# Decode attention by plain fp32 matmuls on four 32-column tiles instead of rounded/rest pairs

## The chip, the core and the metric

The kernel runs on one NeuronCore of a Trainium2 chip. The metric is the device time of one launch in microseconds (us). PE is the matrix engine (TensorE); PEld are its weight loads, which can overlap its matmuls. DVE, ACT and POOL are the vector, scalar and general engines, SP only issues transfers. PE reads from SBUF, where tensors lie on 128 partitions, and writes to PSUM, which has 8 banks of 512 fp32 columns on each partition.

## What is computed

One inference step of a hybrid decoder layer for 256 prompt tokens and 8 decode sequences (one new token each, 2048 tokens in the past). The part that the change touches is the attention of the decode tokens; there are 8 heads in 2 groups of 4, and each group shares one key/value head of 128 numbers.

```python
# compressed branch -> scores of 64-token blocks -> top 16 of them
o_slc = slc_sample(q, kv_slc, cache_slc, page_table, idx, valid, ...)  # 15 past blocks of 64 keys + the new token
o_win, _ = dense_gqa(q, kv_all[:, :, 0], kv_all[:, :, 1], mask, d, slopes)  # the last 512 keys + the new token
# each branch, per head: s = q.k * SCALE - slope * distance; p = softmax(s); o = p @ v
o = g[:, :, 0] * o_cmp + g[:, :, 1] * o_slc + g[:, :, 2] * o_win
y_a = (o * silu(z_a)) @ w_pa
```

The rest of the layer is one large projection of all 264 tokens, compression of the caches, prompt attention, a gated delta rule, and two output projections.

## The kernel before

**The stream of projections.** Most of PE's work is a list `halves` of half units: a 512 KB piece of weights is loaded by SP into a `raw` buffer (4 halves ahead, 3 buffers), split by ACT and DVE into a rounded part `hi` and a rest `lo` (2 halves ahead), and multiplied by the likewise split activations in three matmuls of 264 columns for each of 8 pieces: hi·hi, hi·rest, rest·hi (`three`, tile `acc`). Their operands have the type fp32r, in which one matmul is one pass over the array. A plain fp32 matmul is two records in the trace, and so two weight loads.

**The side work.** Everything else is written as generators. After each half of a half unit (12 matmuls of the stream) `tick` lets every active generator go on to its next `yield`; `yield 3` skips three ticks. Prompt attention (`g_attn`), the decode chain (`g_dec_cmp`, then `g_dec_slc`, then `g_dec_win`), and later the delta rule are such generators. SP and POOL issue in the order of the program; for PE, ACT and DVE the tile framework's scheduler sets the order by its own simulated times, so that side work stands between the matmuls of the stream. PE takes its instructions in the order in which they were written.

**Decode attention, selected branch (`g_dec_slc`).** For each of 8 sequences two indirect transfers on POOL's queue gather 120 rows of 4 KB of keys (tile `gk`), later of values (`gv`); the next sequence's are asked for one sequence ahead. PE transposes the keys (`gtr`), and ACT and DVE take them out of PSUM as a rounded part and a rest (`gkx`). The queries lie in `qm` the same way: 16 blocks, one for each of the 2 heads' groups and 8 sequences, in each of which only the four rows of that group and sequence are not zero. So every matmul adds into all 64 rows (2 groups x 8 sequences x 4 heads) of one score tile `gsc`: `qk` gives one matmul with 128 query columns (rounded and rest) on the rounded keys, and one with 64 on the keys' rest. `scores` adds both halves of the partitions, `row_softmax` works on 64 partitions, `pt_split` transposes the 64 rows of probabilities and splits them again (`sP`). `split1` splits the values (`gvx`), and `pv_part` multiplies: 2 matmuls of 256 columns (both groups' values) for each of 8 key tiles; `pv_take` adds from the result `pvo` only the rows that belong to this group and sequence (a mask `rmask`) to `acc2`.

**Decode attention, window branch (`g_dec_win`).** The same with 512 keys per sequence that come by plain transfers on SP's queue, for two sequences at a time (`wk`, `wv`), and go out again, shifted by a token, to the output cache on POOL's queue (`o_wk`, `o_wv`). Their splits are `wkx` and `wvx`, the scores `wsc`, the probabilities `wP`. At the end two small matmuls (`smo`) bring `acc2` into the order of the output.

All large tiles (`gk`, `gkx`, `gv`, `gvx`, `wk`, `wkx`, ...) share 13 buffers of one pool (`slot`): a new tile waits until the last reader of the tile that had its buffer is done.

Of the kernel before, what the change touches and what calls it, by code (L numbers as in the profile page):

```python
# [10 lines left out]
F32 = mybir.dt.float32  # L11
# [37 lines left out]

def shape_constants():  # L50
# [14 lines left out]
    for t in range(2):  # L65
# [8 lines left out]
    row = np.arange(64)  # L74
    srow = slope[(row // 32) * 4 + row % 4]
    c.add("c64", srow[:, None] * np.arange(64)[None])
    c.add("wrow", srow[:, None] * (np.arange(8) * 64 - 512)[None])
    c.add("e64", (row[None] // 4) == np.arange(16)[:, None])
    c.add("sel", ((row[None, None] // 32) == np.arange(2)[None, :, None])
          & (((row[None, None] // 4) % 8) == np.arange(8)[:, None, None]))  # L80
    c.add("rmask", ((p[:, None] % 64) // 4) == np.arange(16)[None])
# [57 lines left out]
def program(tc, A):  # L139
# [37 lines left out]
    # constants  # L177
# [41 lines left out]
    # long-lived small tiles  # L219
# [14 lines left out]
    grow = cp.tile([64, 2], F32, name="grow")  # L234
# [37 lines left out]
    # ---- x: rms norm, split  # L272
# [36 lines left out]
    # ---- streams  # L309
# [167 lines left out]
    # ---- projections  # L477
# [17 lines left out]
    def g_qstat(h):  # L495
# [7 lines left out]
        if h == 7:  # L503
# [19 lines left out]
            L["qm"] = qm = slot("qm", [128, 2112], F32R)  # L523
            G.memset(qm.bitcast(F32), 0.0)
            qv = qm.rearrange("p (i c) -> p i c", c=132)
            qf = qd.rearrange("p g b r -> p (g b) r")
            S.activation(qv[:, :, 0:4], qf, AF.Copy)
            V.tensor_sub(qv[:, :, 64:68], qf, qv[:, :, 0:4])
# [63 lines left out]
    def g_small(ps):  # L592
# [25 lines left out]
        S.activation(gd, p2[:, 0:64], AF.Copy)  # L618
        for br in range(2):
            mm(p2[0:64, 192 + br:193 + br], x[:, 2 + 2 * br:4 + 2 * br].rearrange("p a b r -> p (a b r)"), ones[0:24, 0:1])  # L620
        V.tensor_copy(grow, p2[0:64, 192:194])
# [8 lines left out]
    # ---- decode: compressed attention, selection, gathers  # L630
    def g_dec_cmp():
# [42 lines left out]
        # ranks  # L674
# [44 lines left out]
        mm(p7[0:64, 0:16], C("e64", 16), vb[:, 1, :])  # L719
        sb_ = cp.tile([64, 16], F32, name="sbias")  # L720
        V.tensor_scalar(sb_, p7[0:64, 0:16], 64.0, -float(PAST), ALU.mult, ALU.add)
        V.tensor_scalar(sb_, sb_, C("c64", 64)[:, 1:2], None, ALU.mult)
# [4 lines left out]
    def new_token(w):  # L727
        yield from wait("q")
        pr = tp.tile([128, 64], F32, name="ntp", tag="a", bufs=NA)
        V.tensor_tensor(pr.rearrange("p (g b r) -> p g b r", g=2, b=NB), qd,  # L730
                        knT[:, w, :, :, None].to_broadcast([128, 2, NB, 4]), ALU.mult)
        yield 3
        pt = psb("ntk")
        mm(pt[0:64, 128:129], pr, ones[:, 0:1])
        for g in range(2):
            mm(pt[0:64, 0:128], C("sel", 8)[:, 64 * g:64 * g + 64], L["kvd"][:, w, 1, g, :], start=g == 0, stop=g == 1)
        sn = tp.tile([64, 8], F32, name="ntm", tag=f"ntm{w}")
        ve = tp.tile([64, 128], F32, name="ntv", tag=f"ntv{w}")
        V.tensor_scalar(sn[:, 0:1], pt[0:64, 128:129], SCALE, None, ALU.mult)
        S.activation(ve, pt[0:64, 0:128], AF.Copy)  # L740
        L["nt", w] = sn, ve
        mark(("nt", w))

    def row_softmax(sc, n, w):
# [11 lines left out]
        V.scalar_tensor_tensor(acc2[0:64], ve, sn[:, 4:5], acc2[0:64], ALU.mult, ALU.add)  # L756

    def scores(out, sc, bias, shape):
        lo = slot("slo", [64, 960])
        lo = lo[:, 0:math.prod(shape)]  # L760
        for k, ps in enumerate(out):
            n = math.prod(shape) // len(out)
            S.activation(lo[:, n * k:n * k + n], ps[64:128, 0:n], AF.Copy, scale=SCALE)
            V.scalar_tensor_tensor(sc[:, n * k:n * k + n], ps[0:64, 0:n], SCALE, lo[:, n * k:n * k + n], ALU.mult, ALU.add)
        V.tensor_add(sc, sc, bias)

    def qk(ps, i, hi, lo, first, last):
        qm = L["qm"]
        a, b = qm[:, 128 * i:128 * i + 128], qm[:, 128 * i:128 * i + 64]
        n = hi.shape[-1]  # L770
        if first:
            mm(ps[:, 0:n], a, hi, start=True, stop=False)
        mm(ps[0:64, 0:n], b, lo, start=False, stop=False)
        if not first:
            mm(ps[:, 0:n], a, hi, start=False, stop=last)

    def pt_split(name, sc, nt, np_):
        pt = psb("ptr")
        for t in range(nt):
            tr(pt[0:np_, 64 * t:64 * t + 64], sc[:, np_ * t:np_ * t + np_])  # L780
        P_ = slot(name, [128, 8, 128], F32R)
        v = pt[0:np_, 0:64 * nt].rearrange("p (t c) -> p t c", t=nt)
        S.activation(P_[0:np_, 0:nt, 0:64], v, AF.Copy)
        V.tensor_sub(P_[0:np_, 0:nt, 64:128], v, P_[0:np_, 0:nt, 0:64])
        return P_

    def pv_part(po, P_, np_, ts, nt, hi, lo):
        for t in ts:
            h = lambda: mm(po[:, 0:256], P_[0:np_, t, :], hi(t), start=t == 0, stop=t == nt - 1)
            if t == 0:  # L790
                h()
            mm(po[0:64, 0:256], P_[0:np_, t, 0:64], lo(t), start=False, stop=False)
            if t:
                h()

    def pv_take(po, b):
        for g in range(2):
            i = 8 * g + b
            V.scalar_tensor_tensor(acc2, po[:, 128 * g:128 * g + 128], C("rmask")[:, i:i + 1], acc2, ALU.mult, ALU.add)

    def split1(name, src, shape, np_=128):
        x = slot(name, [128, 2] + shape, F32R)
        S.activation(x[0:np_, 0], src, AF.Copy)
        V.tensor_sub(x[0:np_, 1], src, x[0:np_, 0])
        return x

    def g_dec_win():
# [30 lines left out]
        def wk_qk(b, x):  # L838
            for g in range(2):
                qk(ps, 8 * g + b, x[:, 0, g], x[:, 1, g], b + g == 0, b * g == 7)  # L840

        prev = None
        for b in range(NB):
            if b % 2 == 0:
                if b < 6:
                    load_k(b // 2 + 1)
                else:
                    load_v(0)
            x = split1("wkx", kr[b // 2][:, b % 2, :, 0:512], [2, 512])
            if prev is not None:  # L850
                yield 3
                wk_qk(b - 1, prev)
            prev = x
        yield 2
        wk_qk(7, prev)
        bb = slot("wb", [64, 2, 512])
        V.tensor_tensor(bb[:, 0].rearrange("p (n m) -> p n m", m=64), C("wrow", 64)[:, :, None].to_broadcast([64, 8, 64]),
                        C("c64", 64)[:, None, :].to_broadcast([64, 8, 64]), ALU.add)
        sc = bb[:, 1]
        yield 7  # L860
        scores([ps], sc, bb[:, 0], [512])
# [3 lines left out]
        P_ = pt_split("wP", sc, 4, 128)  # L865
        def wv_pv(b, x):
            po = PV("pvo")
            pv_part(po, P_, 128, range(4), 4, lambda t: x[:, 0, t], lambda t: x[:, 1, t])
            pv_take(po, b)

        prev = None
        for b in range(NB):
            if b % 2 == 0 and b < 6:
                load_v(b // 2 + 1)
            x = split1("wvx", vr[b // 2][:, b % 2], [4, 256])
            if prev is not None:
                yield
                wv_pv(b - 1, prev)
            prev = x
        yield 5  # L880
        wv_pv(7, prev)
        yield 7
        pt = psb("smo")
        yield 2
        for i in range(2):
            mm(pt[:, 0:64], acc2, ident[:, 64 * i:64 * i + 64], start=i == 0, stop=i == 1)
        V.tensor_add(oD, oD, pt[:, 0:64])
        mark("oD")

    def g_dec_slc():  # L890
        yield from wait("idx")
        yield from wait(("kv", 0), 4)
        G.memset(acc2, 0.0)
# [15 lines left out]
        def gk_qk(b, g, x):  # L909
            for half in range(2):  # L910
                o = slice(480 * half, 480 * half + 480)
                qk(ps[half], 8 * g + b, x[:, 0, o], x[:, 1, o], b + g == 0, b * g == 7)

        prev = None
        for b in range(NB):
            if b < NB - GP:
                kr[b + GP] = gather("gk", "cslk", b + GP)
            elif b - NB + GP < VP:
                vr[b - NB + GP] = gather("gv", "cslv", b - NB + GP)
            for g in range(2):  # L920
                x = slot("gkx", [128, 2, 960], F32R)
                for half in range(2):
                    pt = psb("gtr")
                    for t in range(4):
                        tr(pt[:, 120 * t:120 * t + 120], kr[b][0:120, g, 4 * half + t, :])
                    o = slice(480 * half, 480 * half + 480)
# [3 lines left out]
                if prev:  # L930
                    gk_qk(*prev)
                prev = b, g, x
            del kr[b]
        yield 6
# [785 lines left out]
```

## Time and profile before

| | us |
|---|---|
| median of 3 runs (1165.35 to 1169.48) | 1166.74 |
| profiled execution, span | 1167.3 |
| PE busy | 1135.1 (97%) |
| PE weight loads busy | 1097.8 (94%) |
| DVE busy | 789.7 (68%) |
| ACT busy | 607.6 (52%) |
| POOL busy | 147.5 (13%) |

The page gives no time outside the span, and the span of the profiled execution lies within the spread of the timed runs. A share of busy time is an average over stages; matmuls overlap in their records (one ends while the next has begun), so that what a matmul takes of PE is the distance from its start to the next start, and not its own length. The decode chain's selected branch stands between 388 and 571 us, its window branch between 560 and 664 us.

### The profile page before, as it was taken

How to read it: one execution, taken by the hardware profiler on the slowest of the kernel's cores; microseconds unless marked ns; L12 is line 12 of the kernel's file. 1: busy time of each engine (PE TensorE's matmuls, PEld its weight loads, DVE VectorE, ACT ScalarE, POOL GpSimd, SP SyncE). 2: the span in 40 equal slices, each digit the busy share in tenths (PEclk: the TensorE clock that was granted, in tenths of full speed). 3: DMA queues.
4: the chain of work that ended last, by engine and by line, in shares of the span. 5: the costliest groups of instructions: out<-in, count | busy, mean ns of one | idle time of the engine just before them, and what ended most of it. 6: DMA issues, size and time to landing. Idle time of an engine off the chain costs nothing.

```text
span 1167.3 us, 24685 instructions
## 1 busy us (share of the span) xinstructions
PE 1135.1 (97%) x9136; PEld 1097.8 (94%) x9136; DVE 789.7 (68%) x1651; ACT 607.6 (52%) x1173; POOL 147.5 (13%) x218
## 2 busy tenths in 40 slices
PE   3999999999999999999899999998999999999998
PEld 3989999999999997998899999998998799999998
DVE  3487665443677876986888876899575665567543
ACT  4455655444635776875666554443345354344332
POOL 4420344100001221204112100100100000000000
PEclk9999999999999999999999999999999999999999
DMA  8874576334436865468887644554743345555663
GB/s 296 256 223 148 191 217 203 106 133 164 159 133 198 227 181 147 135 192 210 320 316 269 245 162 162 188 204 134 231 172 118 127 145 179 183 181 210 206 237 128
DMA packets 76844, 222.83 MB, mean 191 GB/s; under 512 B 10465, under 2 KB 27370, under 8 KB 75186
## 3 DMA queue, kind: packets, MB, share of 16 engines
q1 hardware_dynamic: 59922, 168.55, 42.7%
q0 software_dynamic: 14784, 45.68, 13.6%
q10 hardware_dynamic: 2016, 7.01, 1.5%
q8 instruction: 72, 1.18, 0.4%
q14 instruction: 50, 0.41, 0.1%
HBM read 203.21 MB, written 17.99 MB: 189 GB/s over the span
## 4 chain that ended last, share of the span: by engine, by line
PE 82%; DVE 5%; DMA 3%; issue 1%; POOL 1%; ACT 1%; SPq 0%; DVEq 0%; ACTq 0%; POOLq 0%
PE acc L199 66%; PE og L199 2%; DMA gv<-cslv,idx 2%; DVE lo L327 1%; DVE lanes L1234 1%; PE po L199 1%; PE gsc L199 1%; PE gtr L196 1%; PE sw L199 1%; DVE prod L1233 1%; PE ps L199 1%; PE pvo L199 1%; DMA raw<-win 1%; PE dS L199 1%; PE cf L199 1%
## 5 line engine op out<-in xcount | busy, mean ns | idle before, releaser
L326 ACT ACTIVATE hi<-raw 128x1024 fp32r<-128x1024 f32 (+1 forms) x250 | 264.1, 1056 | 324.2 <-PE acc L199 260.5
L199 PE MATMUL acc<-xh,hi 128*128 128x264 f32 (+1 forms) x1488 | 428.5, 288 | 1.4 <-DVE gate L1489 1.0
L199 PE MATMUL acc<-xl,hi 128*128 128x264 f32 (+1 forms) x1488 | 426.6, 287 | 0.0
L199 PE MATMUL acc<-xh,lo 128*128 128x264 f32 (+1 forms) x1488 | 425.9, 286 | 0.0
L327 DVE TENSOR_TENSOR lo<-raw,hi 128x1024 fp32r<-128x1024 f32 (+1 forms) x250 | 304.5, 1218 | 172.1 <-ACT hi L326 168.5
L199 PEld LDWEIGHTS acc<-xh,hi 128*128 128x128 f32 (+1 forms) x1488 | 280.3, 188 | 3.8 <-ACT hi L326 1.2
L199 PEld LDWEIGHTS acc<-xl,hi 128*128 128x128 f32 (+1 forms) x1488 | 280.4, 188 | 1.9 <-issue 0.7
L199 PEld LDWEIGHTS acc<-xh,lo 128*128 128x128 f32 (+1 forms) x1488 | 279.5, 188 | 2.0 <-issue 1.0
L199 PE MATMUL acc<-hi,w1h 128*128 128x254 f32 (+1 forms) x512 | 147.6, 289 | 16.5 <-ACT hi L403 16.5
L199 PE MATMUL acc<-lo,w1h 128*128 128x254 f32 (+1 forms) x512 | 146.4, 286 | 3.8 <-DVE lo L404 3.6
L199 PE MATMUL acc<-hi,w1l 128*128 128x254 f32 (+1 forms) x512 | 144.9, 283 | 0.0
L404 DVE TENSOR_TENSOR lo<-rawc,hi 128x512 fp32r<-128x512 f32 (+2 forms) x136 | 84.0, 656 | 51.1 <-ACT hi L403 45.3
L199 PEld LDWEIGHTS acc<-hi,w1h 128*128 128x128 f32 x512 | 97.8, 191 | 16.8 <-ACT hi L403 16.7
L403 ACT ACTIVATE hi<-rawc 128x512 fp32r<-128x512 f32 (+2 forms) x136 | 74.6, 599 | 58.6 <-PE acc L199 54.4
L199 PEld LDWEIGHTS acc<-lo,w1h 128*128 128x128 f32 x512 | 98.3, 192 | 5.1 <-DVE lo L404 4.9
L199 PEld LDWEIGHTS acc<-hi,w1l 128*128 128x128 f32 x512 | 98.3, 192 | 0.1
L380 POOL DMA_DIRECT2D rawc<-ccmp x125 | 67.4, 539 | 100.4 <-issue 70.0
L199 PE MATMUL acc<-oh,hi 128*128 128x264 f32 x256 | 72.9, 285 | 0.4 <-ACT gate L1482 0.4
L199 PE MATMUL acc<-ol,hi 128*128 128x264 f32 x256 | 72.7, 284 | 0.0
L199 PE MATMUL acc<-mh,hi 128*128 128x264 f32 x256 | 72.6, 284 | 0.0
L199 PE MATMUL acc<-oh,lo 128*128 128x264 f32 x256 | 72.6, 283 | 0.0
L199 PE MATMUL acc<-ml,hi 128*128 128x264 f32 x256 | 72.5, 283 | 0.0
(447 smaller groups left out, 1685.2 us busy)
## 6 DMA issues: line engine op xcount, KB each, us to landing
raw<-win SPq DMA_DIRECT2D x184, 512.0 KB, 3.8
raw<-wpab SPq DMA_DIRECT2D x32, 512.0 KB, 3.2
raw<-wo SPq DMA_DIRECT2D x32, 512.0 KB, 4.3
rawc<-ccmp SPq DMA_DIRECT2D x126, 128.0 KB, 3.1
rawc<-ccmp POOLq DMA_DIRECT2D x125, 128.0 KB, 3.1
raw<-w SPq DMA_DIRECT2D x8, 512.0 KB, 8.0
wk<-winK SPq DMA_DIRECT2D x8, 512.0 KB, 7.4
o_wk<-wk POOLq DMA_DIRECT2D x8, 512.0 KB, 7.8
```

Of the source, the lines that this page charges most:

```text
L196: T.transpose(out, in_, ident[0:n, 0:n])
L199: T.matmul(out, lhsT, rhs, start=start, stop=stop, **k)
L326: S.activation(self.hi, self.raw, AF.Copy)
L327: V.tensor_sub(self.lo, self.raw, self.hi)
L380: e.dma_start(rawc[kv, b][j // 8][:, j % 8].rearrange("p s c g -> p (s c g)"), src[kv, bass.ds(r, 1)].rearrange("o d f -> (o d) f"))
L403: S.activation(h, src, AF.Copy)
L404: V.tensor_sub(l, src, h)
L1233: V.tensor_tensor(pp, Lt[:, 0:i, 0:i], La[:, i, 0:i, None].to_broadcast([64, i, i]), ALU.mult)
L1234: V.tensor_reduce(Lt[:, i, 0:i], pp.rearrange("p j c -> p c j"), AX.X, ALU.add, negate=True)
```

## The change

- The 64 rows become 128: four quadrants of 32 partitions, of which each uses 16. Quadrant j belongs to sequence parity j // 2 and group j % 2; in it, four places of four heads stand for the sequences of that parity. Constants (`c64`, `wrow`, `e64`, `sel`), the new token's scores, the gates and the softmax follow this order; `rmask` goes, `perm` and `gath` come.
- `qm` holds plain fp32 queries. `qk` takes two sequences at a time and gives four matmuls, one for each quadrant, with 32 columns of weights and the keys of one sequence and group as they are. There is no split of keys any more: `gkx` is one fp32 copy (half by ACT, half by DVE), and the window's keys are read where the transfer put them.
- `scores` is one DVE operation for each score tile, with the bias in it. `pt_rows` transposes 128 rows of probabilities and copies them out once.
- `pv_part` multiplies plain fp32 values: 32 columns of probabilities by 128 columns of values, for each key tile and each group; even key tiles go to one quadrant, odd ones to the other. `po` holds four sequences side by side, and `pv_take` copies it out once for four sequences (`X`, one tile for each branch).
- `smo` becomes one matmul with `perm` for the new tokens' part, and 16 with `gath` (8 columns each), which pick each sequence's rows out of `X` and add the two quadrants.

```diff
-            L["qm"] = qm = slot("qm", [128, 2112], F32R)
-            S.activation(qv[:, :, 0:4], qf, AF.Copy)
-            V.tensor_sub(qv[:, :, 64:68], qf, qv[:, :, 0:4])
+            qx = slot("qm", [128, 640])
+            L["qm"] = qm = qx[:, 128:640].rearrange("p (j i c) -> p j i c", j=4, i=4)
...
-    def scores(out, sc, bias, shape):
-        lo = slot("slo", [64, 960])
...
+    def scores(out, sc, bias):
+        n = sc.shape[-1] // len(out)
         for k, ps in enumerate(out):
+            V.scalar_tensor_tensor(sc[:, n * k:n * k + n], ps[:, 0:n], SCALE, bias[:, n * k:n * k + n], ALU.mult, ALU.add)
+
+    def qk(ps, i, keys):
+        for j in range(4):
+            x = keys(j // 2, j % 2)
+            mm(ps[32 * j:32 * j + 32, 0:x.shape[-1]], L["qm"][:, j, i, :], x, start=i == 0, stop=i == 3)
+
+    def pt_rows(name, sc, nt, np_):
+        P_ = slot(name, [128, 8, 128])
+        for t0 in range(0, nt, 4):
+            pt = psb("ptr")
+            for t in range(4):
+                tr(pt[0:np_, 128 * t:128 * t + 128], sc[:, np_ * (t0 + t):np_ * (t0 + t) + np_])
+            S.activation(P_[0:np_, t0:t0 + 4, :], pt[0:np_, :].rearrange("p (t c) -> p t c", t=4), AF.Copy)
         return P_
 
-    def pv_part(po, P_, np_, ts, nt, hi, lo):
+    def pv_part(po, P_, np_, b, ts, nt, val):
+        o = 128 * (b % 4)
         for t in ts:
...
+            for g in range(2):
+                j, c = 2 * g + t % 2, 2 * (b % 2) + g
+                mm(po[32 * j:32 * j + 32, o:o + 128], P_[0:np_, t, 32 * c:32 * c + 32], val(g, t), start=t < 2, stop=t >= nt - 2)
+
+    def pv_take(po, w, b):
+        if b % 4 == 3:
+            S.activation(L["X", w][:, b - 3:b + 1, :], po.rearrange("p (b d) -> p b d", b=4), AF.Copy)
...
     def g_dec_win():
+        for bp in range(4):
+            if bp < 3:
+                load_k(bp + 1)
+            else:
+                load_v(0)
+            yield 3
+            qk(ps, bp, lambda bl, g: kr[bp][:, bl, g, 0:512])
...
+            pv_part(po, P_, 128, b, range(4), 4, lambda g, t: vr[b // 2][:, b % 2, t, 128 * g:128 * g + 128])
+            pv_take(po, 1, b)
...
-        for i in range(2):
-            mm(pt[:, 0:64], acc2, ident[:, 64 * i:64 * i + 64], start=i == 0, stop=i == 1)
+        mm(pt[:, 0:64], acc2, C("perm"), start=True, stop=False)
+        for w in range(2):
+            for b in range(NB):
+                mm(o[:, :, b, :], L["X", w][:, b, :], gx[:, :, b, :], start=False, stop=w * b == 7)
...
     def g_dec_slc():
+            kt[b % 2] = slot("gkx", [128, 2, 960])
             for g in range(2):
-                x = slot("gkx", [128, 2, 960], F32R)
                 for half in range(2):
...
-                    S.activation(x[:, 0, o], pt[:, 0:480], AF.Copy)
-                    V.tensor_sub(x[:, 1, o], pt[:, 0:480], x[:, 0, o])
+                    if half:
+                        V.tensor_copy(o, pt[:, 0:480])
+                    else:
+                        S.activation(o, pt[:, 0:480], AF.Copy)
                     yield
+            if b % 2:
+                yield 2
+                for half in range(2):
+                    qk(ps[half], b // 2, lambda bl, g: kt[bl][:, g, 480 * half:480 * half + 480])
...
             for half in range(2):
-                x = split1("gvx", vr[b][0:120, :, 4 * half:4 * half + 4, :], [2, 4, 128], 120)
+                yield
+                pv_part(po, P_, 120, b, range(4 * half, 4 * half + 4), 8, lambda g, t: vr[b][0:120, g, t, :])
+            pv_take(po, 0, b)
```

Where the instructions stand. First PE, at the scores of the selected branch, before: `gtr` are the keys' transposes, `gsc` the score matmuls (output rows x columns; 64 rows are the matmul on the keys' rest), `ps` is prompt attention.

```order
L196 MATMUL gtr<-cst,gk 128x120 x4
L199 MATMUL gsc<-gkx,qm 64x480
L199 MATMUL gsc<-gkx,qm 128x480
L199 MATMUL ps<-kTa,qT 128x271
L196 MATMUL gtr<-cst,gk 128x120 x4
L199 MATMUL gsc<-gkx,qm 64x480
L199 MATMUL gsc<-gkx,qm 128x480
```

And after, where the first two sequences' score matmuls stand (`pst` and `ps` are prompt attention's, `acc` the stream's):

```order
L207 MATMUL acc<-xh,lo 128x264
L207 MATMUL gsc<-gkx,qm 32x480 x6
L204 MATMUL pst<-cst,zz 128x128 x3
L207 MATMUL gsc<-gkx,qm 32x480
L204 MATMUL gtr<-cst,gk 128x120 x4
L207 MATMUL acc<-xh,hi 128x264
L207 MATMUL acc<-xl,hi 128x264
L207 MATMUL acc<-xh,lo 128x264
L207 MATMUL gsc<-gkx,qm 32x480
```

Before, a rest/rounded pair stood behind each group of transposes; now eight matmuls for two sequences stand together, and here other work cuts the eight into 6, 1 and 1. The four pairs of sequences have them in stretches of 6, 1, 1; 2, 6; 6, 2; and 8. The window's sixteen stand as 4, 4, 4, 2, 2.

Second PE, at the values of the selected branch, before (`pvo` is the product, `cvt` belongs to the delta rule's preparation):

```order
L199 MATMUL cvt<-cst,qsq_8783 128x1 x2
L199 MATMUL pvo<-gvx,sP 64x256 x2
L199 MATMUL pvo<-gvx,sP 128x256
L199 MATMUL pvo<-gvx,sP 64x256
L199 MATMUL pvo<-gvx,sP 128x256
L199 MATMUL pvo<-gvx,sP 64x256
L199 MATMUL pvo<-gvx,sP 128x256
L199 MATMUL acc<-xl,hi 128x264
L199 MATMUL acc<-xh,lo 128x264
```

And after, at the third sequence:

```order
L207 MATMUL acc<-xl,hi 128x264
L207 MATMUL acc<-xh,lo 128x264
L207 MATMUL pvo<-gv,sP 32x128 x8
L207 MATMUL cvt<-cst,qsq_8807 128x1 x2
L207 MATMUL acc<-xh,hi 128x264
L207 MATMUL acc<-xl,hi 128x264
L207 MATMUL acc<-xh,lo 128x264
```

The eight matmuls of half a sequence's key tiles stand together, mostly with 12 matmuls of the stream between one eight and the next; they read the gathered tile `gv` itself. In the selected branch the 128 stand in 19 stretches (2, 6, 8, 7, 1, seven of 8, 1, 7, five of 8), in the window branch the 64 in 10 (4, 1, 7, 4, six of 8).

Third POOL's queue, the value gathers of the sequences 1 to 3 (numbered tiles in rising order) with what they wait for: DMASW are earlier transfers, DVE and PE the last reader of the buffer's former tile. Before:

```order
L900 DMA gv_8826<-cslv,idx_6606 120x1024 [waits DMASW5_49,DMASW6_49,DMASW4_49,DVE_49]
L900 DMA gv_8826<-cslv,idx_6606 120x1024
L900 DMA gv_8856<-cslv,idx_6606 120x1024 [waits DMASW2_49,DMASW1_49,DVE_49]
L900 DMA gv_8856<-cslv,idx_6606 120x1024 [waits DMASW7_49]
L900 DMA gv_8922<-cslv,idx_6606 120x1024 [waits DMASW0_49,PE_49]
```

After:

```order
L892 DMA gv_8799<-cslv,idx_6620 120x1024 [waits DMASW4_49,PE_49,Activation_49]
L892 DMA gv_8799<-cslv,idx_6620 120x1024 [waits DMASW5_49]
L892 DMA gv_8866<-cslv,idx_6620 120x1024 [waits DMASW6_49,DMASW0_49,DMASW7_49,DVE_49,PE_49]
L892 DMA gv_8866<-cslv,idx_6620 120x1024
L892 DMA gv_8915<-cslv,idx_6620 120x1024 [waits DMASW3_49,DMASW2_49,PE_49]
```

Before, sequence 1 took the buffer of `slo` (free when DVE has added up the scores), sequence 2 that of sequence 0's values (free when DVE has split them), and sequence 3 that of prompt attention's keys and values (free when the last `po` is done). Now sequence 1 takes that of the last transposed keys, sequence 2 that of the probabilities' rows `sb` (free when they are transposed), and sequence 3 that of sequence 0's values (free when PE has multiplied them); prompt attention's buffer goes to sequence 5.

## Rows read from the trace of the kernel before

**Rows 1.** The page: the span, and busy time of each engine.
```profile
span 1167.3 us, 24685 instructions
PE 1135.1 (97%) x9136; PEld 1097.8 (94%) x9136; DVE 789.7 (68%) x1651; ACT 607.6 (52%) x1173; POOL 147.5 (13%) x218
```
**Rows 2.** Windows: stretch, length, busy us by engine, granted clock, DMA share, GB/s.
```profile
515.00:572.00 57.00, 52.75 (x376) 47.09 (x375) 40.77 (x72) 33.33 (x47) 17.27 (x15) 0.97 0.81 219
572.00:604.00 32.00, 32.00 (x238) 30.03 (x237) 27.61 (x56) 20.89 (x33) 6.92 (x10) 1.00 0.97 366
```
**Rows 3.** PE's timeline (start, length, what): the stream, old score and value matmuls.
```profile
388.06 0.29 PE L199 MATMUL acc<-xh,lo 128*128 128x264 f32 x1
388.18 0.38 PE L199 MATMUL gsc<-gkx,qm 128*128 128x480 f32 x1
388.40 0.28 PE L199 MATMUL acc<-xh,hi 128*128 128x264 f32 x1
...
568.54 2.04 PE L199 MATMUL pvo<-gvx,sP 120*128 120x256 f32 x16
...
572.23 1.09 PE L199 MATMUL wsc<-wkx,qm 128*128 128x512 f32 x4
```
**Rows 4.** PE's timeline: plain fp32 matmuls on part of the array, and the whole array again.
```profile
872.06 0.28 PE L199 MATMUL acc<-xh,lo 128*128 128x264 f32 x1
872.27 1.16 PE L199 MATMUL dS<-aT,ktk 64*128 64x128 f32 x8
873.36 0.39 PE L199 MATMUL acc<-xh,hi 128*128 128x264 f32 x1
873.58 0.28 PE L199 MATMUL acc<-xl,hi 128*128 128x264 f32 x1
...
903.83 0.28 PE L199 MATMUL acc<-xh,hi 128*128 128x264 f32 x1
904.04 1.96 PE L199 MATMUL vn<-prod,wT 128*64 128x128 f32 x16
905.93 0.65 PE L196 MATMUL vnb<-cst,dvn 128*128 128x128 f32 x4
```
**Rows 5.** PE's timeline: plain fp32 matmuls of 512 columns, whole array.
```profile
527.51 3.70 PE L199 MATMUL po<-PTt,kTa 128*128 128x512 f32 x8
```
**Rows 6.** Timeline of PE: the 32x32 tiles, all 16 passes; the first two alone.
```profile
836.32 0.44 PE L199 MATMUL inv<-P,prod 32*32 32x32 f32 x16
836.32 0.22 PE L199 MATMUL inv<-P,prod 32*32 32x32 f32 x2
```
**Rows 7.** Groups by line: the old end of the decode chain, and the splits of gathered data.
```profile
L199 PE MATMUL smo<-cst,acc 128*128 128x64 f32 x4 | 0.6, 261 | 0.0
...
L804 DVE TENSOR_TENSOR gvx<-gv,gvx 120x1024 fp32r<-120x1024 f32 x16 | 19.3, 1221 | 11.1 <-ACT gvx L803 9.6 <-issue 1.5
```
**Rows 8.** PE's timeline where it stood idle, and the windows around it.
```profile
551.35 1.18 PE L199 MATMUL pvo<-gvx,sP 120*128 120x256 f32 x8 [1.13 <-DVE qss L1124]
559.32 1.19 PE L199 MATMUL pvo<-gvx,sP 120*128 120x256 f32 x8 [1.71 <-DVE acc L799]
563.30 0.61 PE L199 MATMUL cvt<-cst,qsq 128*128 128x1 f32 x4 [1.36 <-ACT qsq L1119]
567.93 0.42 PE L199 MATMUL acc<-xh,hi 128*128 128x264 f32 x1
568.15 0.42 PE L199 MATMUL acc<-xl,hi 128*128 128x264 f32 x1
540.00:550.00 10.00, 9.95 (x83) 9.74 (x81) 7.82 (x12) 6.59 (x9) 5.83 (x5) 1.00 1.02 230
560.00:570.00 10.00, 8.64 (x60) 8.43 (x59) 9.54 (x21) 6.98 (x9) 1.47 (x2) 0.83 0.78 256
```
**Rows 9.** POOL's timeline: value gathers, in brackets the idle time before and what ended it.
```profile
519.74 0.97 POOL L900 DMA_INDIRECT gv<-cslv,idx  x1 [25.39 <-DVE gvx L804]
531.51 1.17 POOL L900 DMA_INDIRECT gv<-cslv,idx  x1 [9.08 <-PE po L199]
```

More of the change, by code (lines that the diff above doesn't have):

```diff
@@ L233, in program @@
     gd = cp.tile([128, 64], F32, name="gd")
-    grow = cp.tile([64, 2], F32, name="grow")
+    grow = cp.tile([128, 2], F32, name="grow")
     acc2 = cp.tile([128, 128], F32, name="acc2")
@@ L618, in g_small @@
         S.activation(gd, p2[:, 0:64], AF.Copy)
+        xp = tp.tile([24, 2, 2, 2, 32], F32, name="gxp", tag="a", bufs=NA)
+        V.memset(xp, 0.0)
         for br in range(2):
-            mm(p2[0:64, 192 + br:193 + br], x[:, 2 + 2 * br:4 + 2 * br].rearrange("p a b r -> p (a b r)"), ones[0:24, 0:1])
-        V.tensor_copy(grow, p2[0:64, 192:194])
+            for c in range(2):
+                V.tensor_copy(xp[:, br, c, :, 0:16].rearrange("p g (i r) -> p g i r", r=4),
+                              x[:, 2 + 2 * br:4 + 2 * br].rearrange("p a (i c) r -> p c a i r", c=2)[:, c])
+            mm(p2[:, 192 + br:193 + br], xp[:, br].rearrange("p c g x -> p (c g x)"), ones[0:24, 0:1])
+        V.tensor_copy(grow, p2[:, 192:194])
         V.tensor_scalar(beh, smt[:, :, 64:72], 0.5, None, ALU.mult)
@@ L718, in g_dec_cmp @@
         p7 = psb("dsl")
[L719 to L722, printed above, removed]
+        mm(p7[:, 0:16], C("e64", 16), vb[:, 1, :])
+        sb_ = cp.tile([128, 16], F32, name="sbias")
+        V.tensor_scalar(sb_, p7[:, 0:16], 64.0, -float(PAST), ALU.mult, ALU.add)
+        V.tensor_scalar(sb_, sb_, C("c64")[:, 1:2], None, ALU.mult)
         L["sbias"] = sb_
@@ L728, in new_token @@
         yield from wait("q")
-        pr = tp.tile([128, 64], F32, name="ntp", tag="a", bufs=NA)
-        V.tensor_tensor(pr.rearrange("p (g b r) -> p g b r", g=2, b=NB), qd,
-                        knT[:, w, :, :, None].to_broadcast([128, 2, NB, 4]), ALU.mult)
+        pr = tp.tile([128, 128], F32, name="ntp", tag="a", bufs=NA)
+        V.memset(pr, 0.0)
+        for c in range(2):
+            o = lambda t: t[:, 64 * c:64 * c + 64].rearrange("p (g x) -> p g x", g=2)[:, :, 0:16].rearrange(
+                "p g (i r) -> p g i r", r=4)
+            V.tensor_tensor(o(pr), o(L["qdp"]), knT[:, w].rearrange("p g (i c) -> p c g i", c=2)[:, c, :, :, None]
+                            .to_broadcast([128, 2, 4, 4]), ALU.mult)
         yield 3
         pt = psb("ntk")
[L734 to L740, printed above, removed]
+        mm(pt[:, 128:129], pr, ones[:, 0:1])
+        for j in range(4):
+            o = slice(32 * j, 32 * j + 32)
+            mm(pt[o, 0:128], C("sel", 8)[:, o], L["kvd"][:, w, 1, j % 2, :])
+        sn = tp.tile([128, 8], F32, name="ntm", tag=f"ntm{w}")
+        ve = tp.tile([128, 128], F32, name="ntv", tag=f"ntv{w}")
+        V.tensor_scalar(sn[:, 0:1], pt[:, 128:129], SCALE, None, ALU.mult)
+        S.activation(ve, pt[:, 0:128], AF.Copy)
         L["nt", w] = sn, ve
@@ L767, in qk @@
[L767 to L784, printed above, removed]
-        return P_
@@ L787, in pv_part @@
-    def pv_part(po, P_, np_, ts, nt, hi, lo):
+        if w:
+            V.scalar_tensor_tensor(acc2, ve, sn[:, 4:5], acc2, ALU.mult, ALU.add)
+        else:
+            V.tensor_scalar(acc2, ve, sn[:, 4:5], None, ALU.mult)
+    def scores(out, sc, bias):
+        n = sc.shape[-1] // len(out)
+        for k, ps in enumerate(out):
+            V.scalar_tensor_tensor(sc[:, n * k:n * k + n], ps[:, 0:n], SCALE, bias[:, n * k:n * k + n], ALU.mult, ALU.add)
+    def qk(ps, i, keys):
+        for j in range(4):
+            x = keys(j // 2, j % 2)
+            mm(ps[32 * j:32 * j + 32, 0:x.shape[-1]], L["qm"][:, j, i, :], x, start=i == 0, stop=i == 3)
@@ L837, in g_dec_win @@
         yield 3
[L838 to L858, printed above, removed]
+        for bp in range(4):
[5 more added lines that the diff above has]
+            qk(ps, bp, lambda bl, g: kr[bp][:, bl, g, 0:512])
+        bb = slot("wb", [128, 2, 512])
+        V.tensor_tensor(bb[:, 0].rearrange("p (n m) -> p n m", m=64), C("wrow")[:, :, None].to_broadcast([128, 8, 64]),
+                        C("c64")[:, None, :].to_broadcast([128, 8, 64]), ALU.add)
         sc = bb[:, 1]
         yield 7
-        scores([ps], sc, bb[:, 0], [512])
+        scores([ps], sc, bb[:, 0])
         yield
@@ L864, in g_dec_win @@
         yield 4
[L865 to L871, printed above, removed]
+        P_ = pt_rows("wP", sc, 4, 128)
+        L["X", 1] = slot("X1", [128, NB, 128])
         for b in range(NB):
@@ L908, in g_dec_slc @@
         yield 20
[L909 to L914, printed above, removed]
+        kt = {}
         for b in range(NB):
```

101 lines of the change are left out of this document (37 added, 64 removed).

## The prediction

> **What bounds the kernel now.** I read the page first: of a span of 1167.3 us PE is busy 1135.1, DVE 789.7, ACT 607.6 [rows 1]. So I went to the stretches that the change touches, in the table of windows. In the window branch's key stage PE is busy 32.00 of 32.00 us, while the DMA engines are at .97 [rows 2]. In the selected branch's value stage, 515 to 572 us, PE is busy only 52.75 of 57.00, and the granted clock is .97 [rows 2]. Then I read PE's timeline for what one matmul costs, and where PE stood idle in that stage. The reader should see two things: almost everywhere each pass added to or taken from PE moves the end by its own time, and in one short stage PE waits for DVE and ACT, which wait for gathered values.
>
> **What one pass costs.** A record is longer than the distance to the next start: for the stream's matmul .28 against .12, for an old score matmul .38 against .22 (388.18 to 388.40), in both by .16 [rows 3]. So I take (length - .16) / count for a run of equal passes. That gives (1.09 - .16)/4 = .23 for an old window score, (2.04 - .16)/16 = .1175 for an old value matmul [rows 3], (1.96 - .16)/16 = .1125 for one pass of a plain fp32 matmul of 128 columns (vn) [rows 4], and (3.70 - .16)/8 = .4425 for one of 512 columns (po) [rows 5]. A plain fp32 matmul is two such passes. A pass of 480 columns is then .4425 x 480/512 = .415.
>
> **Old and new matmuls.** What goes: 64 score matmuls x .22 = 14.1, 32 window scores x .23 = 7.4, 192 value matmuls x .1175 = 22.6, together 44.1 us of PE. What comes are 32, 16 and 192 plain fp32 matmuls, each in a tile of 32 columns of the array. One after the other they would take 64 x .415 + 32 x .4425 + 384 x .11 = 26.6 + 14.2 + 42.2 = 83.0. So the change pays only if tiles run beside each other, and how far they do decides the sign.
>
> No row of this kernel has four tiles side by side. The nearest is inv, which uses two 32x32 tiles in turn: 16 passes of 32 columns take (.44 - .16)/16 = .0175 each, where vn's rate gives .1125 x 32/128 = .028 for one; and its first two passes are in a record of .22 together [rows 6], so the second did not wait for the first. That is 1.6 times the rate of one tile, of 2 possible. From this I take tiles as independent queues: four run together, and a stretch lasts as long as its fullest tile. I take no loss, since in inv a pass is hardly longer than the load of its weights, and the new passes are 4 to 15 times as long. The ends of this cost are the full overlap, and none (the 83.0).
>
> By the new order the eight score matmuls of a pair of sequences, which take the four quadrants in turn, stand in stretches of 6, 1, 1; 2, 6; 6, 2; and 8. In six or eight of them the fullest tile has two matmuls, in one or two it has one: (2+1+1) + (1+2) + (2+1) + 2 = 12 matmuls deep, or 24 passes x .415 = 10.0. The window's 4, 4, 4, 2, 2 give 5 matmuls: 10 x .44 = 4.4. The values' 29 stretches give 52: 104 x .11 = 11.4. Together 25.8.
>
> **Change of tile shape.** Around dS, from the start of the stream matmul ahead (872.06) to that of the second one behind (873.58), 1.52 pass; two stream matmuls (.24) and eight passes (.90) are work, so .38 are lost for going into another tile shape and back [rows 4]. Around vn it is 903.83 to 904.04 (.09 over .12) and 904.04 to 905.93 (1.89 for passes worth 1.80), and about .10 on going back, as behind dS: .28 [rows 4]. vn's weights are 64 columns wide and dS's 128; the new ones are 32. I take .31, with .28 and .38 as ends. Of 42 stretches two adjoin transposes in the same tile shape: 40 x .31 = 12.4 (11.2 to 15.2). For the staggered start of four tiles I add one of inv's steps per stretch, 42 x .0175 = .7.
>
> Sum so far: 25.8 + 12.4 + .7 - 44.1 = -5.2.
>
> **The end of the decode chain.** smo was 4 passes [rows 7] and becomes 17 plain matmuls, 34 passes, most of them with 128 columns of weights and 8 of data. The nearest row is dS, whose weights are as wide and whose passes take .11 [rows 4]: +30 x .11 = +3.3 (from +.8, by inv's .0175 a pass, 34 x .0175 + .16 [rows 6], to +3.3). PE is not idle ahead of it [rows 7], so all of it counts.
>
> **DVE and ACT.** The splits go: 16 of gathered values cost DVE 19.3 [rows 7], and others at ACT and for the keys. Where PE is busy throughout, this is worth nothing. It is worth something in 515 to 572: there PE stood idle 1.13, 1.71 and 1.36, together 4.2, ahead of three instructions for DVE or ACT [rows 8]. Behind it the granted clock of 560 to 570 is .83: at the 1.2 GHz level a stream matmul takes .22 (567.93 to 568.15) instead of .12 [rows 8]; .17 of 10 us lost at half speed is 3.4 us at that level, in which 1.7 of work were lost. So the stage holds 5.9. What made DVE and ACT late there were gathers: POOL waited 25.39 us for DVE's split (gvx) before the gather of sequence 2, and 9.08 for PE's po before that of sequence 3 [rows 9]. In the new order sequence 2's waits for the transposes of the probabilities, and sequence 3's for PE's product of sequence 0, both earlier; and the gathered tile goes to PE with no split between. What is late next is PE's own stream. I take -5.0, with 0 and -5.9 as ends.
>
> The remaining edits I cost at nothing. The window's keys are read where they land, and DMA at .97 there [rows 2] could hold PE up; but the copies that stood between are gone, so each transfer gains their time, and PE was busy throughout with it. The score additions, the copies of `X` and the second copy of the transposed probabilities fall on DVE and ACT, of which DVE was busy 40.77 of 57 us [rows 2] and loses more than it gets; without that cover PE would wait for each as long as for a split, 1.22 [rows 7]. The constants grow by 176 columns, 90 KB; at the 219 GB/s of [rows 2] that is .4 us, beside other transfers.
>
> **Sum:** -5.2 + 3.3 - 5.0 = -6.9, so the span goes from 1167.3 to 1160.4. The median of the runs is .6 under the profiled span: 1160.
>
> **Rivals.** First, the passes keep the order of the program: the second pass of a tile's matmul waits for the first, and the next tile, which starts behind it, can only run beside that second pass. Then a stretch of n matmuls takes n + 1 passes' time: (32 + 8) x .415 + (16 + 5) x .4425 + (192 + 29) x .11 = 16.6 + 9.3 + 24.3 = 50.2. With 12.4 for the shapes this is +18.5 instead of -5.2, and with +3.3 and -5.0 the time is 1184. For it speaks that PE takes everything else in its order; against it that inv's first pass does not stand alone [rows 6]. From an overlap of 2.5 on (83.0 / 2.5 = 33, against 44.1 - 12.4 - .7 - 3.3 + 5.0 = 32.7) the change gains; this rival has 1.65.
>
> The Trainium skill has a rule that speaks for this rival: "TensorE: Matmul & The Clock Gate", section "Part 3: Packing small matmuls", under "The mechanism", says that matmuls start and end in the order of the program. The total of inv's 16 passes agrees with it as well (8 matmuls in turn on two tiles: 9 passes' time, 9 x .028 = .25, of .28 measured); only the first two passes speak against it. By the rule the time would be this rival's 1184.
>
> Second, tiles that lie on the same 128 rows don't run together at all, and 83.0 + 12.4 - 44.1 = +51.3 come, which makes 1217. inv's tiles lie on different rows, so no row excludes it.
>
> Third, no change that can be measured (3.5 us, .3%, is about what a measurement of this kernel can tell). Either the waits of 515 to 572 stay, because the gathers are limited by the DMA engines (share 1.02 in 540 to 550 [rows 8]) and not by their buffers: 1165. Or the four tiles overlap no better than inv's, at 1.6 of 2: 25.8 / .81 = 31.9, which is 6.1 more, 1166.5.
>
> The same section, under "Measured speedup vs the span model", gives 2.38 for three column tiles of another type, 79% of full. The size agrees with inv's rows; by it the time would be about 1167, and no run here shows four fp32 tiles.
>
> **How the numbers follow.** The forecast gets .47, the third rival .18, the first .20, the second .15. The likeliest's own range is 1155 to 1166: with the shapes at .28, smo at +.8 and all of the stage it is 1160.4 - 1.2 - 2.5 - .9 = 1155.8, less the .6; with nothing of the stage 1165.4. The range goes 2 us, about the distance of the runs of before from their median, below that, to 1153, and over the first rival to 1185; it leaves the second one out. Faster gets .48 (the forecast, and .01 of the third, whose 1165 is not far from the bound), same the other .17, slower the two rivals' .35.
>
> **What would show it.** In the new profile the matmuls of a stretch's four quadrants should start within hundredths of each other, and eight value matmuls should take about .45 us (two deep in each tile, so 4 x .11) and not 1.0 (first rival, 9 x .11) or 1.8 (second, 16 x .11). A score stretch of 6 should take 1.7. The start of the first stream matmul behind a stretch should be late by about .2. smo should take 3.7. In the value stage PE should be idle less than 1 us with the clock at 1.00, and POOL should no longer wait 25 us before a value gather. I am wrong if the eight value matmuls take over .6, or if the idle time of that stage stays.

## The result, and the profile after

| | us | ratio to before, 95% interval |
|---|---|---|
| before, median | 1166.49 | |
| after, median of 4 runs (1176.49 to 1178.77) | 1176.77 | 1.0088 [1.0072, 1.0104] |
| forecast | 1160 (1153 to 1185) | |

The kernel became slower by 10 us, where 7 less was forecast. The page of the kernel after, span and busy times, as in [rows 1]:

```profile
span 1174.8 us, 24964 instructions
PE 1138.8 (97%) x9366; PEld 1083.1 (92%) x9366; DVE 735.2 (63%) x1581; ACT 571.8 (49%) x1126; POOL 140.2 (12%) x217
```

I read first what the change touches. PE's timeline after, at one stretch of eight score matmuls, in it the first pass of four quadrants alone, and a stretch of eight value matmuls (compare the old ones in [rows 3]):

```profile
485.82 0.28 PE L207 MATMUL acc<-xh,lo 128*128 128x264 f32 x1
486.03 1.82 PE L207 MATMUL gsc<-gkx,qm 128*32 128x480 f32 x16
487.78 0.39 PE L207 MATMUL acc<-xh,hi 128*128 128x264 f32 x1
...
486.03 0.61 PE L207 MATMUL gsc<-gkx,qm 128*32 128x480 f32 x4
...
531.89 0.64 PE L207 MATMUL pvo<-gv,sP 120*32 120x128 f32 x16
532.47 0.39 PE L207 MATMUL acc<-xh,hi 128*128 128x264 f32 x1
```

Sixteen passes of 480 columns take 1.75 us from start to next start, where one after the other they would take 16 x .415 = 6.6. The first four passes, one for each quadrant, lie in one record of .61, which is hardly longer than one pass with its latency. Sixteen value passes take .58. The four tiles run side by side nearly in full: four passes deep at .415 each would be 1.66.

The windows of the kernel after in the value stage, as in [rows 2], and then around the end of the decode chain:

```profile
515.00:572.00 57.00, 57.00 (x555) 45.89 (x554) 23.24 (x49) 22.80 (x38) 13.01 (x15) 1.00 0.87 252
...
632.00:636.00 4.00, 4.00 (x39) 4.00 (x37) 1.56 (x2) 1.96 (x4) 0.00 (x0) 1.00 0.98 273
636.00:640.00 4.00, 4.00 (x21) 4.00 (x21) 1.26 (x7) 0.43 (x2) 0.00 (x0) 0.54 0.59 195
640.00:644.00 4.00, 4.00 (x24) 4.00 (x23) 0.00 (x0) 0.39 (x1) 0.00 (x0) 0.61 0.00 0
```

PE no longer stands idle in the value stage (57.00 of 57.00, before 52.75 [rows 2]), and the clock there is 1.00. But behind smo, from 636 to 644 us, the granted clock is .54 and .61. PE's timeline there:

```profile
633.21 3.57 PE L207 MATMUL smo<-cst,X 128*128 128x8 f32 x30
636.63 1.85 PE L207 MATMUL dec<-smt,cst 128*128 128x8 f32 x8
...
638.70 0.42 PE L207 MATMUL acc<-xl,hi 128*128 128x264 f32 x1
638.92 0.42 PE L207 MATMUL acc<-xh,lo 128*128 128x264 f32 x1
```

Matmuls of the stream come .22 apart there (638.70 to 638.92), which is the 1.2 GHz level. Up to here the kernel after is still ahead: the instruction behind its 4901st stream matmul starts at 761.1 us, before at 766.9, so 5.8 sooner. All of the loss, 13.3 us, comes behind that, nearly all of it within 100 us, in the delta rule, of which the change touches no line: from the 4901st to the 5800th stream matmul the kernel after takes 198.8 us, the one before 185.5. PE's waits of the kernel after from 770 to 830 us (what waited for what: us in all, times, longest), and the windows there:

```profile
PE sw L207 <- DMA sst<-stS: 9.7, 1, 9.7
PE acc L207 <- DVE gate L1466: 2.2, 2, 1.6
PE acc L207 <- ACT hi L334: 1.0, 1, 1.0
```

```profile
800.00:806.00 6.00, 5.49 (x46) 5.28 (x44) 5.90 (x5) 0.39 (x1) 0.65 (x1) 1.00 0.01 3
806.00:816.00 10.00, 0.82 (x4) 0.82 (x5) 0.14 (x1) 0.10 (x1) 4.70 (x8) 0.72 0.69 206
816.00:826.00 10.00, 10.00 (x56) 10.00 (x56) 4.18 (x7) 7.46 (x18) 0.00 (x0) 0.60 0.89 223
```

`sst` is a tile of the delta rule's old state for the decode tokens; `sw` multiplies it. PE waits 9.7 us for its load, and then works at a granted clock of .60. From 800 to 806 the DMA engines stand nearly still (.01): the weights of the stream don't come either. SP's queue says why. First its waits in the kernel after, 780 to 830 us, then its issues:

```profile
SPq L1391 <- DMA td<-lanes: 19.0, 2, 17.7
SPq L329 <- DVE lo L335: 16.5, 6, 3.2
```

```profile
810.08 0.33 SPq L1391 DMA_DIRECT2D sst<-stS  x1
810.50 0.38 SPq L329 DMA_DIRECT2D raw<-win  x1
```

And SP's issue of the first `sst` in the kernel before:

```profile
775.90 0.42 SPq L1414 DMA_DIRECT2D sst<-stS  x1
```

SP stood 19.0 us at the load of `sst`, until POOL's transfers had taken `lanes` away, and everything behind it in SP's queue, the weights first, stood with it. `lanes` is the tile of a row-by-row recurrence on DVE that ends at 805 us. The order of the two programs shows the wait (numbered tiles; DMASW are transfers of POOL's queue). Before and after:

```
681 L1414 DMA sst_12107<-stS 128x2048
```

```
687 L1391 DMA sst_12149<-stS 128x2048 [waits DMASW3_49,DMASW4_49,DMASW2_49,DMASW7_49,DVE_49,PE_49]
```

Two tiles of the delta rule, the first `sst` and `U`, are asked for about the same time, when one buffer of the pool is free (that of `qT`) and the next to come free is that of `lanes`. Before, `sst` came first and got `qT`'s, and `U`, which holds the result of `lanes`, got that of `lanes`. Afterwards `U` came first. `sst` is asked for by the decode part of the delta rule behind a fixed `yield 88`; `U` by its main part, which starts once the decode chain has marked its end, and that chain has fewer yields now (`dec`, the main part's first matmul, starts at 636.63 us, before at 645.4). So nobody moved `sst`; the generator beside it came sooner.

### The profile page after: what moved, and what is told of

It reads as the page before. It is cut to its first block, busy times and chain, and to the rows that moved or that the text cites. A ratio compares the mean times of both kernels' runs of the same rounds, so it can differ in the third digit from the quotient of the medians.

```text
span 1174.8 us, 24964 instructions
## 1 busy us (share of the span) xinstructions
PE 1138.8 (97%) x9366; PEld 1083.1 (92%) x9366; DVE 735.2 (63%) x1581; ACT 571.8 (49%) x1126; POOL 140.2 (12%) x217
## 4 chain that ended last, share of the span: by engine, by line
PE 86%; DVE 5%; DMA 2%; issue 1%; ACT 0%; POOL 0%; DVEq 0%; SPq 0%; POOLq 0%
PE acc L207 69%; PE og L207 2%; DVE lanes L1211 2%; PE sw L207 2%; DVE lo L335 1%; PE po L207 1%; PE pvo L207 1%; PE gtr L204 1%; DMA wv<-winV 1%; PE ps L207 1%; PE gsc L207 1%; DVE prod L1210 1%; PE dS L207 1%; PE cf L207 1%; PE uw L207 1%
## 5 line engine op out<-in xcount | busy, mean ns | idle before, releaser
L207 PE MATMUL acc<-xh,hi 128*128 128x264 f32 (+1 forms) x1488 | 434.0, 292 | 1.5 <-ACT hi L334 1.0
```

The source lines that it names most:

```text
L207: T.matmul(out, lhsT, rhs, start=start, stop=stop, **k)
```

## The experiments

Theory B: the buffer of `sst` costs the 13 us. Rival D: the recurrence on DVE is late anyhow. The experiments from e3 on concern the forecast's terms. Each kernel was timed on one chip in turn with the kernel before; ratios are to that.

**e1.** In the changed kernel:

```diff
-        yield 88
+        yield 70
```

> The changed kernel, in which the decode part of the delta rule asks for its first state tile (sst) after 70 ticks instead of 88, so that it gets the free buffer of qT as in the kernel before, and U gets that of lanes. Theory B (buffer): sst's load, put behind the end of the lanes recurrence by the buffer, holds up SP's queue and so PE for 9.7 us, and the low clock behind it costs some 3.5 more; with this edit the idle time of 9.7 goes, PEclk stays 1.00 there, and the time falls by 13 from 1176.8 to 1162 to 1165, which is 1 to 4 faster than before. Rival D (DVE): the lanes recurrence, on which DVE is busy without a break until 805 us, is late in any case, and PE waits for its result elsewhere: at most the 3.5 of the clock come back, 1173 or more.

Measured: 1163.54 (ratio .9976 [.9961, .9991]), 13.2 less than the changed kernel. SP issues `sst` without a wait, and the same three windows read:

```profile
759.87 0.71 SPq L1391 DMA_DIRECT2D sst<-stS  x1
```

```profile
800.00:806.00 6.00, 6.00 (x48) 6.00 (x48) 5.70 (x13) 2.12 (x2) 0.54 (x1) 0.92 0.77 194
806.00:816.00 10.00, 10.00 (x85) 10.00 (x84) 6.17 (x8) 2.79 (x4) 3.92 (x6) 1.00 0.90 278
816.00:826.00 10.00, 9.53 (x80) 9.32 (x79) 5.29 (x7) 4.51 (x5) 0.00 (x0) 1.00 0.82 222
```

The DMA engines work on (.77 instead of .01), PE is busy, the clock is above .9. Rival D falls: it allowed 1173 or more. From the 4901st to the 5800th stream matmul e1 takes 186.5 us (198.8 in the changed kernel), so 12.3 of the 13.9 us between the two spans come from there. The other 1.6 stand ahead of it, behind smo, where the clock was low for a shorter time (see e6).

**e2.** The same the other way round, in the kernel before:

```diff
-        yield 88
+        yield 92
```

> The kernel before, with 92 ticks instead of 88, so that sst is asked for behind U and gets the buffer of lanes, as in the changed kernel. Theory B: +9 to +14, 1176 to 1181, with one idle time of PE of 7 to 10 us ahead of sw and a granted clock under .8 behind it. Rival D: within 3 us of before, 1164 to 1169.

Measured: 1190.38 (ratio 1.0198 [1.0169, 1.0226]). PE's wait from 790 to 860 us, and SP's from 780 to 830:

```profile
PE sw L199 <- DMA sst<-stS: 22.2, 1, 22.2
```

```profile
SPq L1414 <- DMA td<-lanes: 30.8, 1, 30.8
```

Four ticks, without any other edit, cost the old kernel 23 us by the same wait. The size was more than I expected, 9 to 14: SP runs into the load at 781 us here and at 791 in the changed kernel, and both get it away at 810 to 812, so SP stands longer (30.8 against 19.0). Theory B's mechanism holds; its price depends on how long ahead of the end of `lanes` SP runs into it.

**e9.** e1 changes two things, the buffer and the time of the load. So here the load stays where the changed kernel has it, and only the buffer is taken sooner, by a memset of one column:

```diff
-        yield 88
+        yield 70
+        s0 = slot("sst", [128, 2, 8, 128])
+        V.memset(s0[:, 0, 0, 0:1], 0.0)
+        yield 18
         for b0 in range(0, NB, 2):
-            ss = slot("sst", [128, 2, 8, 128])
+            ss = s0 if b0 == 0 else slot("sst", [128, 2, 8, 128])
```

> The changed kernel with sst's load where it stands in it, behind 88 ticks and at the same place in SP's queue; only its buffer is taken 18 ticks earlier, by a memset of one column, so that it is qT's and not that of lanes. Theory B (buffer): the load waits for nothing, the idle time of 9.7 us ahead of sw goes as in e1, 1162 to 1166. Rival E (what helped in e1 is that the load and all that hangs on it came 18 ticks sooner): PE still waits for sst or for what follows it by 5 us or more, 1171 to 1177.

Measured: 1167.29 (ratio 1.0007 [.9995, 1.0019]), a little above the range of theory B. The wait is gone from the trace: SP issues the load without one, and PE's waits from 770 to 830 us are:

```profile
788.73 0.42 SPq L1394 DMA_DIRECT2D sst<-stS  x1
...
PE inv L207 <- DMA U<-td: 2.6, 1, 2.6
PE acc L207 <- DVE gate L1469: 2.0, 4, 0.8
```

By the ratios the buffer alone gives back 1.0088 - 1.0007, .81% or 9.4 us. The remaining .31% to e1 is 3.6 us, with 2.2 either way by the two intervals, and its cause is not shown. Rival E would put it down to the time of the load, but the trace shows no price of that: from the 4901st to the 5800th stream matmul e9 takes 186.5 us, as e1 does. The execution that was profiled was the fastest of ten, span 1160.4, so where the others lost time no trace shows.

**e3.** e1 with the matmuls of a stretch written quadrant by quadrant:

```diff
-        for t in ts:
-            for g in range(2):
-                j, c = 2 * g + t % 2, 2 * (b % 2) + g
+        for j in range(4):
+            for t in [t for t in ts if t % 2 == j % 2]:
+                g = j // 2
+                c = 2 * (b % 2) + g
```

and the same for the score matmuls.

> The kernel of e1 with the matmuls of a stretch written quadrant by quadrant (all of the first, then all of the second, ...) instead of in turn. Theory Q (each tile is a queue of its own, whatever the order in the program): eight value matmuls stay at .57 us and the time within 2 us of e1. Rival F (matmuls start in the order of the program, and only neighbours on different tiles run together): eight value matmuls take 13 passes, 1.4 us, eight score matmuls 5.2 instead of 1.75, and the time is 25 to 40 us over e1, about 1195.

Measured: 1164.53 (ratio .9976 [.9961, .9991]), as e1. PE's timeline at a stretch of eight value matmuls, and its first four passes alone:

```profile
530.48 0.66 PE L207 MATMUL pvo<-gv,sP 120*32 120x128 f32 x16
531.07 0.39 PE L207 MATMUL acc<-xh,hi 128*128 128x264 f32 x1
...
530.48 0.34 PE L207 MATMUL pvo<-gv,sP 120*32 120x128 f32 x4
```

The stretch takes .59 (531.07 - 530.48) instead of .58. Four passes still start together, though now the program has all four passes of a tile one after the other; on one tile alone such passes come .117 apart (1.87 / 16, e8). So in stretches of this length tiles are queues of their own, and the rule by which each matmul starts behind the one ahead of it in the program (the prediction's first rival) did not hold between tiles here; the Trainium skill states it ("TensorE: Matmul & The Clock Gate", "Part 3: Packing small matmuls — row/col tiling"), and the starts of e3 speak against it, so the measurement decides.

**e8.** What the overlap is worth: e1 with every value matmul in the first quadrant (`po[0:32]`, one group of sums).

> The kernel of e1 with all value matmuls in the first quadrant (the sums of the four fall together, so what is computed is not attention). The price of the tiles' overlap: if tiles run together fully and one tile takes its passes one by one, 384 passes instead of 104 deep, 280 x .11 = +31 us, 1194; eight matmuls take 1.8 us instead of .57. If the overlap is smaller than the starts in the trace show, less.

Measured: 1196.06 (ratio 1.0246 [1.0213, 1.0278]), in two runs. PE's timeline at eight matmuls:

```profile
518.06 1.93 PE L207 MATMUL pvo<-gv,sP 120*32 120x128 f32 x16
519.93 0.39 PE L207 MATMUL acc<-xh,hi 128*128 128x264 f32 x1
```

1.87 instead of .58, and summed over the trace the value matmuls take 45.6 us instead of 15.2: +30.4, as forecast from 280 passes x .11. By the ratios the time is 31.5 over e1.

**e4.** Whether the splits, or the gathers' buffers, made PE idle in the value stage: e1 with a copy in two steps put back.

```diff
+                src = vr[b][0:120, :, 4 * half:4 * half + 4, :]
+                x = slot("gvx", [128, 2, 2, 4, 128])
+                S.activation(x[0:120, 0], src, AF.Copy)
+                V.tensor_tensor(x[0:120, 1], src, x[0:120, 0], ALU.max)
                 yield
```

> The kernel of e1 with the gathered values copied before PE reads them, by ACT and then DVE, as the rounded part and the rest were made before (the result is a copy and the matmuls stay as they are). Theory S (the split between gather and matmul made PE wait in the value stage): idle time of 2 to 5 us comes back between 505 and 560 us, and the time is 3 to 7 over e1. Rival G (it was the buffers for which the gathers waited): the idle time stays under 1 us and the time within 2 of e1.

Measured: 1172.02 (ratio 1.0040 [1.0023, 1.0057]), 8.5 over e1 (7.5 by the ratios), a little more than theory S allowed. PE's waits from 500 to 620 us:

```profile
PE pvo L207 <- DVE gvx L946: 3.9, 5, 2.5
PE ptr L204 <- DVE wb L778: 1.1, 1, 1.1
```

Waits for the copied values are back, 3.9 us with a longest of 2.5, where e1 has none at `pvo`: a copy on the way from gather to PE is enough to make PE idle there. That the gathers' buffers alone would not have done, this run does not exclude in full, since the tiles `gvx` take buffers as well. It also doesn't show which edit took away the three waits of before, for those name DVE's `qss` and `acc` and ACT's `qsq` [rows 8] and not the split. Of the rest, 2.0 us are idle time in the window branch behind it, and the clock is lower there (.91 from 600 to 620 us) and for longer behind smo (see e6).

**e6 and e5.** The low clock behind smo. e6 is e1 with smo in four parts:

```diff
             for b in range(NB):
+                if b % 4 == 0:
+                    yield
                 mm(o[:, :, b, :], L["X", w][:, b, :], gx[:, :, b, :], start=False, stop=w * b == 7)
```

> The kernel of e1 with smo's 16 matmuls in four parts of four, with 12 stream matmuls between them. Theory W: smo's own time stays 3.6 us or grows to 4, but the clock stays 1.00 from 628 to 650, 1.5 to 2 less than e1. Rival O: the clock falls to .6 to .7 for 4 us somewhere behind smo as in e1, and the time is that of e1.

Measured: 1159.65 (ratio .9942 [.9920, .9964]). Its windows, and behind them those of e1 over the same times:

```profile
636.00:640.00 4.00, 4.00 (x37) 4.00 (x36) 1.18 (x1) 0.49 (x1) 0.00 (x0) 1.00 0.58 213
640.00:644.00 4.00, 4.00 (x36) 4.00 (x36) 3.54 (x16) 1.44 (x5) 0.00 (x0) 1.00 0.19 37
```

```profile
636.00:640.00 4.00, 4.00 (x25) 4.00 (x25) 1.22 (x7) 0.42 (x2) 0.00 (x0) 0.64 0.70 237
640.00:644.00 4.00, 4.00 (x33) 4.00 (x32) 0.90 (x1) 1.06 (x1) 0.00 (x0) 0.93 0.02 4
```

With twelve stream matmuls between each four of smo the clock stays 1.00, so it was the long row of small matmuls that lowered it (theory W). All six kernels that were traced with this row in one piece show the low clock at its end or right behind it, at a price of 1.7 us of work (e1) to 5.1 (e3), and 3.4 in the changed kernel, e4, e8 and e9; e5, e6 and e7, which break the row up, do not. The spans of e6 and e1 differ by 3.8 (1157.1 against 1160.9), but 2.1 of that stand ahead of the 1000th stream matmul, long before the edit; from the 3200th to the 4300th, where the edit is, e6 is 1.5 faster, about the 1.7 that the clock explains. The intervals of the ratios overlap, so the time alone would not prove it. e5 lets DVE add the two branches first, so that 8 matmuls do, in two parts:

```diff
+        V.tensor_add(L["X", 1], L["X", 1], L["X", 0])
+        yield 2
```

> The kernel of e1, in which DVE first adds the two branches' X, so that smo has 8 matmuls with gath instead of 16, in two parts with stream matmuls between. Theory W (smo's 34 passes cost their own 3.6 us and behind them a stretch at the 1.2 GHz level, 636 to 642 us): smo falls to 2.0 us, PEclk from 632 to 648 stays 1.00, and the time falls by 3 to 4 from e1's 1163.5 to 1160. Rival O (smo costs its own time alone, the low clock comes from what stands behind it): 1.8 less, the clock falls as in e1.

Measured: 1159.74 (ratio .9932 [.9910, .9955]), the clock 1.00 from 628 to 652 us, smo's own time 1.8 us (3.6 in e1).

**e7.** Fewer changes of tile shape: e5 with the value matmuls of a whole sequence, or of two in the window branch, without a `yield` between.

> The kernel of e5 with the value matmuls of a whole sequence (selected branch) or of two (window branch) in one stretch: 19 stretches instead of 28. If each change of tile shape costs .31, as read from dS and vn, the time falls by 9 x .31 = 2.8 below e5; rival: the longer stretches hold up the stream's evacuation or wait for gathers, and it is no faster or up to 3 slower.

Measured: 1156.17 (ratio .9904 [.9888, .9921]), 3.6 below e5, for 10 stretches fewer (29 to 19; nearly all of them in the selected branch, since the window branch still has 9 of its 10). The two intervals overlap, so the traces say more: from the 3200th to the 4300th stream matmul e7 takes 181.54 us and e5 184.18, which is 2.6 less, .26 for each stretch where .31 was assumed. One of the longer stretches on PE's timeline:

```profile
530.97 1.08 PE L207 MATMUL pvo<-gv,sP 120*32 120x128 f32 x32
531.98 0.39 PE L207 MATMUL acc<-xh,hi 128*128 128x264 f32 x1
```

Sixteen matmuls take 1.01 (531.98 - 530.97) where twice eight took 1.16 and one more change of shape. The .43 between 1.01 and .58 is for four more passes in each tile, .11 a pass; so of a stretch's .58 some .14 are not passes. By the ratios this kernel is 11 us faster than the kernel before and 21 faster than the changed one.

## Why the prediction was wrong

The direction was wrong, by a cost that stands in no term of the sum; the terms themselves came out near.

- **Old and new matmuls with the tile shapes, -5.2.** Right, and somewhat too small. Adding up the distances from start to next start, the old stretches took 48.2 with the excess on the matmuls around them, 2.0 of which is the transposes' change of shape that now falls on the stream; the new ones 38.5: -7.7. Full overlap was the right choice of the two ends. The rivals that rest on less overlap were wrong, by e3 and e8. Eight value matmuls take .58 where .45 was forecast, by the .14 that a stretch takes beside its passes (e7).
- **smo, +3.3.** Right as its own time (3.8 against .4), too small by what follows it: from 636 to 644 us the granted clock lacks .46 and .39 of full speed, and (.46 + .39) x 4 = 3.4 us of work are lost. By e6 that is the row's doing, and its size is not fixed: 1.7 in e1. The row that could have warned me was [rows 8], where the clock was low behind idle time; I took only idle time for its cause, and here PE was never idle.
- **The value stage, -5.0.** Right in size: the idle time of 4.2 and the low clock are gone, and POOL's longest wait before a value gather is 14.15 us instead of 25.39 [rows 9]. That the split was the cause fits e4 but is not shown alone: the buffers changed with it.
- Together -7.7 + 3.8 - .4 + 3.4 - 4.2 - 1.7 = -6.8; the trace shows -5.8 behind the 4901st stream matmul. A microsecond is not accounted for.
- **The step that failed** is "the remaining edits I cost at nothing". Among them are the edits that take yields out of the decode chain and tiles out of the pool. I followed their effect on the gathers of this chain alone, and asked of no tile behind it which buffer it gets. The bill came 170 us behind the end of the chain, +13.3, and by e1, e2 and e9 it was the buffer that `sst` got: idle times of 9.7 and 3.1 in 770 to 836 us, where before there were 4.1 in smaller pieces, sw at the lower clock (17.8 us instead of 14.3 for its 128 passes) and stream matmuls with it. The order of the new program had it in one row, the load of `sst` with six waits where before there was none, on SP, ahead of the stream's weights.
- **The rival on the other side** that I set (1184, by overlap) was slower for a reason that didn't hold; that the time lies in the range is luck.

## What to carry to other kernels

Where a pool of shared buffers serves generators that run at their own pace, an edit that shortens one of them can change which tile gets which buffer in all that follow; compare the waits of every load in the order before and after, on in-order queues above all, also far behind the edit. A load that waits for a buffer on the queue that feeds the main stream holds up everything behind it (here SP stood 19.0 us and the DMA engines nearly stood still), so take its buffer early (e9) or put it where its buffer is free (e1). Plain fp32 on four column tiles ran here at 3.0 times the rate of one for the values (45.6 / 15.2, e8) and by estimate 3.8 times for the scores (6.6 / 1.75), and fewer changes of tile shape gained a little more (e7).

## What the runs showed of the hardware

Four column tiles on the same 128 rows ran their fp32 passes beside each other nearly without loss (16 passes of 480 columns in 1.75 us, four of them deep 1.66), also where the program had them tile by tile (e3). A row of 34 passes with full weights and mostly 8 columns, 3.8 us with only two other passes in it and no idle time, was followed by nearly 7 us at the 1.2 GHz level (8 us at a mean granted clock of .575); the same row cost 1.7 to 5.1 us of work in the five other kernels that have it, and in four parts with stream matmuls between them the granted clock stayed 1.00 (e6).
